# One layer of a hybrid diffusion backbone: weights split into high and low parts in operations of 1024 columns, in two pairs of buffers

## The chip, the cores and the metric

The kernel runs on one core of a Trainium2 chip. The metric is the time of one execution in device microseconds (us), lower is better. Engines are named as in the profile: PE (TensorE matmul), PEld (its weight load), DVE (VectorE), ACT (ScalarE), POOL (GpSimd), SP (the queue that issues most DMAs).

## What is computed

One layer is run over 128 context tokens and 256 latent tokens (384 in all) of width 2048, in fp32:

```python
h = rmsnorm(x, g_pre_mix) * (1.0 + sc1) + sh1
q, k, v, f, uv, ga, gf, gc = split(h @ w_in)              # 2048 x 10752
merged = (sigmoid(ga) * (attention(q, k, v) @ w_br_a)
        + sigmoid(gf) * (fourier(f) @ w_br_f)
        + sigmoid(gc) * (gating(uv) @ w_br_c))
x = x + gt1 * rmsnorm(merged @ w_out, g_post_mix)
h = rmsnorm(x, g_pre_mlp) * (1.0 + sc2) + sh2
x = x + gt2 * rmsnorm(square(relu(h @ w1)) @ w2, g_post_mlp)   # 2048 x 8192 x 2048
# sh1, sc1, gt1, sh2, sc2, gt2 = silu(c) @ w_ada + b_ada, for the context's and the latents' vector
```

## The kernel before

**Every weight is read once and used in three products.** A product is made in the type fp32r from two parts of each operand, a rounded high part and the remainder (low part): high weight by high activation, high by low, low by high. The two parts of a weight are made on the chip by `split` (line 70): ACT rounds it (`whi`, line 71), DVE subtracts the rounded value (`wlo`, recorded under line 65, the helper `tt`).

**The stream.** All weights stand in one list, `stream`, in the order of use. An entry is 128 partitions by up to 1024 columns (512 KB), read by one DMA of SP into a buffer `raw` (line 96, three buffers, `R_BUFS`; at the start six others, the tiles `era` and `erb`). Entries marked "W" are split and multiplied by PE; entries marked "D" are multiplied with the conditioning vector on DVE (line 274, four operations of 512 columns; early ones on PE, line 248), and are needed only later. D entries stand between W entries in three places: corrections for v and f in the first part of the projections, then 96 entries of `w_ada` beside the gates, branches and the output projection (positions 62 to 196 of `main`), then 32 in the MLP.

**Halves.** A W entry gives two halves of 512 columns. Each half has its own pair of tiles, `whi` and `wlo` (lines 117 and 118, four of each, `H_BUFS`). `next_half` (line 124) hands out the next half, and first calls `advance` until two more halves stand ready behind it. So in the program's order the split of an entry stands just ahead of the matmuls on the first half of the entry before it. The four tiles are used in turn: a half's split waits until PE has finished the half four places earlier, and the `raw` buffer becomes free, and with it the DMA three entries later, when the second subtraction is done.

**Blocks.** `blockA` multiplies with the weight as the stationary operand (a half is 12 matmuls of 384 or 386 columns), `blockB` with the weight as the moving one (9 matmuls of 512 columns). Behind each half a `slot` emits one to three pieces of other work (evacuations, attention, norms), so these stand in the queues of ACT, DVE and PE between the splits. Each engine works its queue in order. The first 24 entries of the MLP are only 512 columns wide and give one half each; between them DVE and ACT make the MLP's input (lines 1175 to 1186).

Of the kernel before, what the change touches and what calls it, by code (L numbers as in the profile page):

```python
# [14 lines left out]
F32R = mybir.dt.float32r  # L15
# [4 lines left out]
P = 128  # L20
# [15 lines left out]
def hybrid_layer_kernel(ctx: ExitStack, tc: tile.TileContext, I: dict, O: dict):  # L36
# [5 lines left out]
    wp = ctx.enter_context(tc.tile_pool(name="wp", bufs=3))  # L42
# [21 lines left out]
    def tt(eng, out, a, b, op):  # L64
        eng.tensor_tensor(out=out, in0=a, in1=b, op=op)  # L65

    def f32(ap):
        return ap.bitcast(F32)

    def split(full, hi, lo):  # L70
        nc.scalar.copy(out=hi, in_=full)  # L71
        tt(nc.vector, lo, full, f32(hi), ALU.subtract)

    R_BUFS = 3
    H_BUFS = 4
    RED_AFTER = 14
    ADD_AFTER = 7
    N_EARLY = 6
    stream = []
    state = {"done": 0, "dma": 0}  # L80
    halves = deque()
# [9 lines left out]
    def emit_dma(i):  # L91
        _, w, k0, nk, c0, nc_ = stream[i][:6]
        if i < early["n"]:
            raw = early_raw[i % N_EARLY]
        else:
            raw = wp.tile([P, 1024], F32, tag="raw", name=f"raw{i}", bufs=R_BUFS)
        nc.sync.dma_start(
            out=raw[:, :nk * nc_].rearrange("p (k n) -> p k n", k=nk),
            in_=ktv(w)[:, k0:k0 + nk, c0:c0 + nc_],
        )  # L100
        raws[i] = raw

    def advance():
        i = state["done"]
        if i < early["n"]:
            last_dma = min(i + N_EARLY - 1, early["n"] + R_BUFS - 1)
        else:
            last_dma = i + R_BUFS - 1
        while state["dma"] <= min(last_dma, len(stream) - 1):
            emit_dma(state["dma"])  # L110
            state["dma"] += 1
        e = stream[i]
        state["done"] += 1
        raw = raws.pop(i)
        if e[0] == "W":
            for hf in range(e[3] * e[5] // 512):
                hi = wp.tile([P, 512], F32R, tag="whi", name=f"whi{i}_{hf}", bufs=H_BUFS)
                lo = wp.tile([P, 512], F32R, tag="wlo", name=f"wlo{i}_{hf}", bufs=H_BUFS)
                split(raw[:, hf * 512:(hf + 1) * 512], hi, lo)
                halves.append((hi, lo))  # L120
        else:
            e[6](raw)

    def next_half():
        while not halves:
            advance()
        h = halves.popleft()
        while len(halves) < H_BUFS - 2 and state["done"] < len(stream):
            advance()
        return h  # L130

# [21 lines left out]
    def WB(w, k0, nkt, c0):  # L153
        return [("W", w, k, 2, c0, 512) for k in range(k0, k0 + nkt, 2)]
# [282 lines left out]
    for qd in range(4):  # L437
# [6 lines left out]
        for n in range(4):  # L444
            e = WB(w2, 16 * qd, KT, 512 * n)
# [160 lines left out]
    def blockA(name, src, nkt, evac, k_off=0, width=TOK):  # L606
        ps = [acc_tile(f"{name}_{n}") for n in range(2)]
        for k in range(0, nkt, 2):
            h = next_half()
            mmA(ps, h, k_off + k, src, k == 0, k == nkt - 2, width)  # L610
            slot()
        late.extend(evac(ps))

    def blockB(name, src, nkt, evac, k_off=0):
        ps = [acc_tile(f"{name}_{t}") for t in range(NT)]
        for k in range(nkt):
            h = next_half()
            mmB(ps, h, k_off + k, src, k == 0, k == nkt - 1)
            slot()
        late.extend(evac(ps))  # L620
# [50 lines left out]
    for ch in SCHED:  # L671
        if ch in "sW":
            advance()
            for _ in range(3):
                if xtask:
                    xtask.popleft()()
        elif ch in "Cc":
            consume()
            if ch == "C":
                consume()  # L680
        elif ch == "h" and todo:
            todo.popleft()()
        elif ch == "H":
            while todo:
                todo.popleft()()
# [447 lines left out]
    for k in range(0, KT - 2, 2):  # L1133
        mmA(ps7, next_half(), k, src_m, k == 0, False)
        slot()
    flush()
    hi, lo = (x.rearrange("p (k n) -> p k n", k=2) for x in next_half())
# [166 lines left out]
    for t in range(NT):  # L1304
# [4 lines left out]
        for n in range(4):  # L1309
            c = slice(512 * n, 512 * (n + 1))  # L1310
            o = accn[:, t, c].rearrange("p (k n) -> p k n", n=P)
# [50 lines left out]
```

## Time and profile before

| | |
|---|---|
| median of 3 runs | 2242.39 us (2242.16 to 2245.22) |
| span of the profiled execution | 2241.9 us |
| PE busy | 2168.3 us (97%) |
| DVE busy | 1458.1 us (65%) |
| ACT busy | 814.8 us (36%) |
| bytes moved by DMA | 387.29 MB, 173 GB/s in the mean |

The profile gives one execution; its span reaches from the first to the last instruction and lies 0.5 us below the median of the runs. Busy time of an engine is a union: a matmul is recorded at some 340 ns, though the next one starts 175 ns after it, so the number of matmuls in a stretch says more about PE than its busy share. "Idle before" an instruction is time in which its engine waited for what is named behind the arrow.

### The profile page before, as it was taken

Reading aid. Unit: us, or ns where it says so; the run is one execution under the profiler, and the core shown is the slowest. Engines: PE = TensorE matmul, PEld = TensorE weight load, DVE = VectorE, ACT = ScalarE, POOL = GpSimd, SP = SyncE. Lnnn points to the kernel's source line nnn. Section 1 sums busy time; section 2 is a strip of 40 time slices with the busy share of each in tenths; the row PEclk is TensorE's granted clock in tenths of the full one; section 3 lists DMA queues with packets and bytes.
Section 4 is the critical chain, followed back from the end, with each engine's and each line's share of the span. In section 5 each row is a group of like instructions: output and inputs, shape, how many; then the busy total and the mean of one; then the engine's idle time right before and its main releaser. Section 6 shows DMA issues by size and latency. Waiting matters only on the chain.

```text
span 2241.9 us, 30677 instructions
## 1 busy us (share of the span) xinstructions
PE 2168.3 (97%) x11479; PEld 1988.6 (89%) x11479; DVE 1458.1 (65%) x2331; ACT 814.8 (36%) x1602; POOL 252.6 (11%) x167
## 2 busy tenths in 40 slices
PE   7999899999999998999999999999999999999998
PEld 3679888999899998998989988899889998899986
DVE  4445675558998898989977577787444444345454
ACT  3332334533223232323245443344333443334441
POOL 0000221011222122212212001111000000000000
PEclk9999999999999999999999999999999999999999
DMA  8897753336666765666634466665444444444452
GB/s 309 288 314 232 198 161 123 103 116 196 201 195 194 212 207 168 201 203 224 218 102 134 126 191 200 205 188 174 127 132 124 128 125 129 126 130 123 123 175 88
DMA packets 284405, 387.29 MB, mean 173 GB/s; under 512 B 16156, under 2 KB 184304, under 8 KB 283872
## 3 DMA queue, kind: packets, MB, share of 16 engines
q1 hardware_dynamic: 275952, 372.82, 53.6%
q10 hardware_dynamic: 6192, 6.77, 1.0%
q0 software_dynamic: 2112, 5.74, 0.9%
q8 instruction: 90, 1.47, 0.3%
q14 instruction: 59, 0.48, 0.1%
HBM read 377.94 MB, written 8.26 MB: 172 GB/s over the span
## 4 chain that ended last, share of the span: by engine, by line
PE 75%; DVE 9%; DMA 8%; issue 5%; ACT 1%; POOL 1%; DVEq 0%; ACTq 0%; POOLq 0%; SPq 0%
PE m L576 7%; PE m L577 7%; PE m L575 7%; PE z L599 7%; PE z L600 7%; PE z L598 7%; DMA raw<-in_w_in_dram 4%; DVE wlo L65 4%; PE g L577 3%; PE g L575 3%; PE g L576 3%; DVE adr L274 3%; DMA raw<-in_w_ada_dram 2%; PE sc L248 2%; PE ew L598 1%
## 5 line engine op out<-in xcount | busy, mean ns | idle before, releaser
L65 DVE TENSOR_TENSOR wlo<-raw,whi 128x512 fp32r<-128x512 f32 x908 | 649.7, 734 | 573.5 <-ACT whi L71 566.2
L71 ACT CAST whi<-raw 128x512 fp32r<-128x512 f32 x908 | 547.8, 620 | 1102.8 <-PE z L600 262.0
L598 PE MATMUL z<-whi,ff 128*128 128x512 f32 x720 | 280.1, 389 | 0.0
L599 PE MATMUL z<-wlo,ff 128*128 128x512 f32 x720 | 280.1, 389 | 0.0
L600 PE MATMUL z<-whi,ff 128*128 128x512 f32 x720 | 280.1, 389 | 0.0
L274 DVE SCALAR_TENSOR_TENSOR adr<-raw,silT,adr 128x512 f32<-128x512 f32 x360 | 266.8, 801 | 15.5 <-DMA raw<-in_w_ada_dram 15.4
L577 PE MATMUL g<-hA,wlo 128*128 128x384 f32 x768 | 261.5, 341 | 15.6 <-DVE wlo L65 15.3
L575 PE MATMUL g<-hA,whi 128*128 128x384 f32 x768 | 260.9, 340 | 10.5 <-ACT whi L71 10.5
L576 PE MATMUL g<-hA,whi 128*128 128x384 f32 x768 | 259.4, 338 | 0.0
L575 PE MATMUL m<-h2a,whi 128*128 128x386 f32 x512 | 175.1, 342 | 2.1 <-ACT h2a L1181 2.1
L576 PE MATMUL m<-h2a,whi 128*128 128x386 f32 x512 | 174.3, 340 | 1.1 <-DVE h2a L1185 1.0
L577 PE MATMUL m<-h2a,wlo 128*128 128x386 f32 x512 | 173.8, 339 | 0.0
L577 PEld LDWEIGHTS g<-hA,wlo 128*128 128x128 f32 x768 | 146.2, 190 | 22.1 <-DVE wlo L65 22.1
L600 PEld LDWEIGHTS z<-whi,ff 128*128 128x128 f32 x720 | 135.1, 188 | 28.0
L598 PEld LDWEIGHTS z<-whi,ff 128*128 128x128 f32 x720 | 135.1, 188 | 27.9
L599 PEld LDWEIGHTS z<-wlo,ff 128*128 128x128 f32 x720 | 135.1, 188 | 27.9
L575 PEld LDWEIGHTS g<-hA,whi 128*128 128x128 f32 x768 | 146.1, 190 | 11.5 <-ACT whi L71 11.4
L576 PEld LDWEIGHTS g<-hA,whi 128*128 128x128 f32 x768 | 146.2, 190 | 0.0
L281 POOL PARTITION_ALL_REDUCE adr<-adr x24 | 87.4, 3640 | 302.8 <-DVE adr L274 235.1
L576 PEld LDWEIGHTS m<-h2a,whi 128*128 128x128 f32 x512 | 97.3, 190 | 2.3 <-DVE h2a L1185 2.1
L575 PEld LDWEIGHTS m<-h2a,whi 128*128 128x128 f32 x512 | 97.1, 190 | 2.4 <-ACT h2a L1181 2.3
L577 PEld LDWEIGHTS m<-h2a,wlo 128*128 128x128 f32 x512 | 96.9, 189 | 0.0
(343 smaller groups left out, 3824.6 us busy)
## 6 DMA issues: line engine op xcount, KB each, us to landing
raw<-in_w_mlp_dram SPq DMA_DIRECT2D x244, 512.0 KB, 3.7
raw<-in_w_in_dram SPq DMA_DIRECT2D x156, 512.0 KB, 3.8
raw<-in_w_ada_dram SPq DMA_DIRECT2D x128, 512.0 KB, 4.5
erb<-in_w_ada_dram SPq DMA_DIRECT2D x37, 512.0 KB, 5.5
raw<-in_w_out_dram SPq DMA_DIRECT2D x32, 512.0 KB, 4.2
era<-in_w_ada_dram SPq DMA_DIRECT2D x27, 512.0 KB, 5.1
era<-in_w_in_dram SPq DMA_DIRECT2D x20, 512.0 KB, 5.4
raw<-in_w_br_a_dram SPq DMA_DIRECT2D x16, 512.0 KB, 3.6
```

The costliest lines, as they stand in the source:

```text
L65: eng.tensor_tensor(out=out, in0=a, in1=b, op=op)
L71: nc.scalar.copy(out=hi, in_=full)
L248: nc.tensor.matmul(ps[g:g + 2, :wd], silT[:, :, k], r, start=k < 4, stop=k >= KT - 4)
L274: nc.vector.scalar_tensor_tensor(out=acc[v], in0=r, scalar=vec[:, v, k:k + 1], in1=acc[v], op0=ALU.mult, op1=ALU.add)
L281: nc.gpsimd.partition_all_reduce(out, acc, P, bass_isa.ReduceOp.add)
L575: nc.tensor.matmul(out, wh, xh, start=start, stop=False)
L576: nc.tensor.matmul(out, wh, xl, start=False, stop=False)
L577: nc.tensor.matmul(out, wl, xh, start=False, stop=stop)
L598: nc.tensor.matmul(ps[t], xh, hi, start=first, stop=False)
L599: nc.tensor.matmul(ps[t], xh, lo, start=False, stop=False)
L600: nc.tensor.matmul(ps[t], xl, hi, start=False, stop=last_)
```

## The change

An entry of 1024 columns is split whole: one rounding on ACT and one subtraction on DVE, into one pair of tiles of 1024 columns. There are two such pairs in place of four of 512; they take the same memory. The two halves that are handed out are views of one pair. Two entries of 512 columns share a pair, and each is split for itself into its half of it. The number of halves that stand ready ahead is 2 as before, under a name of its own.

```diff
-    H_BUFS = 4
+    H_TILES = 2
+    AHEAD = 2
...
         if e[0] == "W":
-            for hf in range(e[3] * e[5] // 512):
-                hi = wp.tile([P, 512], F32R, tag="whi", name=f"whi{i}_{hf}", bufs=H_BUFS)
-                lo = wp.tile([P, 512], F32R, tag="wlo", name=f"wlo{i}_{hf}", bufs=H_BUFS)
-                split(raw[:, hf * 512:(hf + 1) * 512], hi, lo)
-                halves.append((hi, lo))
+            n = e[3] * e[5]
+            if "pair" in state:
+                pair, o = state.pop("pair"), 512
+            else:
+                pair, o = [wp.tile([P, 1024], F32R, tag=t, name=f"{t}{i}", bufs=H_TILES) for t in ("whi", "wlo")], 0
+                if n == 512:
+                    state["pair"] = pair
+            split(raw[:, :n], *(t[:, o:o + n] for t in pair))
+            for c in range(o, o + n, 512):
+                halves.append(tuple(t[:, c:c + 512] for t in pair))
...
-        while len(halves) < H_BUFS - 2 and state["done"] < len(stream):
+        while len(halves) < AHEAD and state["done"] < len(stream):
```

DVE's queue beside the gates and branches (`wlo190_0` is the first half of entry 190, `adr` the sums of a D entry, `sig` the gated branches), before:

```order
L65 TENSOR_TENSOR wlo190_0_4721<-raw190_4674,whi190_0_4720 128x512
L65 TENSOR_TENSOR wlo190_1_4725<-raw190_4674,whi190_1_4724 128x512
L271 TENSOR_SCALAR adr_4313<-raw191_4712,silT_89 128x512 x2
L274 SCALAR_TENSOR_TENSOR adr_4313<-raw191_4712,silT_89,adr_4313 128x512 x2
L65 TENSOR_TENSOR wlo192_0_4768<-raw192_4718,whi192_0_4767 128x512
L65 TENSOR_TENSOR wlo192_1_4772<-raw192_4718,whi192_1_4771 128x512
L65 TENSOR_TENSOR sig00_4382<-b0_1_0_4672,sig00_4382 128x384
L65 TENSOR_TENSOR sig01_4396<-b0_1_1_4673,sig01_4396 128x384
L274 SCALAR_TENSOR_TENSOR adr_4313<-raw193_4759,silT_89,adr_4313 128x512 x4
```

and now:

```order
L65 TENSOR_TENSOR wlo190_4313<-raw190_4270,whi190_4312 128x1024
L277 TENSOR_SCALAR adr_3945<-raw191_4304,silT_89 128x512 x2
L280 SCALAR_TENSOR_TENSOR adr_3945<-raw191_4304,silT_89,adr_3945 128x512 x2
L65 TENSOR_TENSOR wlo192_4356<-raw192_4310,whi192_4355 128x1024
L65 TENSOR_TENSOR sig00_4006<-b0_1_0_4268,sig00_4006 128x384
L65 TENSOR_TENSOR sig01_4020<-b0_1_1_4269,sig01_4020 128x384
L280 SCALAR_TENSOR_TENSOR adr_3945<-raw193_4347,silT_89,adr_3945 128x512 x4
```

Two rows have become one of twice the width; nothing else has moved. ACT's queue changes in the same way, from 1556 rows to 1086, as DVE's from 2020 to 1550.

PE's queue at the border between the two halves of entry 192 (lines 575 to 577 are the three products of `mm3`, now 581 to 583), before:

```order
L576 MATMUL b2_1_1_4802<-oC_3836,whi192_0_4767 128x384
L577 MATMUL b2_1_1_4802<-oC_3836,wlo192_0_4768 128x384
L575 MATMUL b2_1_0_4801<-oC_3836,whi192_1_4771 128x384
L576 MATMUL b2_1_0_4801<-oC_3836,whi192_1_4771 128x384
L577 MATMUL b2_1_0_4801<-oC_3836,wlo192_1_4772 128x384
```

and now:

```order
L582 MATMUL b2_1_1_4386<-oC_3516,whi192_4355 128x384
L583 MATMUL b2_1_1_4386<-oC_3516,wlo192_4356 128x384
L581 MATMUL b2_1_0_4385<-oC_3516,whi192_4355 128x384
L582 MATMUL b2_1_0_4385<-oC_3516,whi192_4355 128x384
L583 MATMUL b2_1_0_4385<-oC_3516,wlo192_4356 128x384
```

The order of the matmuls is the same; both halves now read one pair of tiles, which becomes free behind the last matmul of the second half.

ACT's queue at the first entries of the MLP, which are 512 columns wide (lines 1181 and 1187 make the MLP's input `h2a`), before:

```order
L71 CAST whi410_0_10194<-raw410_10098 128x512
L71 CAST whi411_0_10216<-raw411_10116 128x512
L1181 ACTIVATE h2a_10158<-xT2_10168,A2_92 128x128
L1181 ACTIVATE h2a_10158<-xT2_10168,A2_92 128x256
L71 CAST whi412_0_10238<-raw412_10192 128x512
```

and now:

```order
L71 CAST whi410_9264<-raw410_9170 128x512
L71 CAST whi410_9264<-raw411_9188 128x512
L1187 ACTIVATE h2a_9228<-xT2_9238,A2_92 128x128
L1187 ACTIVATE h2a_9228<-xT2_9238,A2_92 128x256
L71 CAST whi412_9306<-raw412_9262 128x512
```

The instructions are the same; entries 410 and 411 now share the pair `whi410`.

## Rows read from the trace of the kernel before

**Rows 1.** Windows by stretch: length, PE, PEld, DVE, ACT, POOL; clock, DMA share, GB/s.

```profile
168.00:290.00 122.00, 111.94 (x619) 107.39 (x618) 79.25 (x134) 37.22 (x71) 19.64 (x22) 0.97 0.71 211
290.00:550.00 260.00, 259.57 (x1453) 245.37 (x1452) 159.53 (x287) 107.57 (x227) 31.15 (x26) 1.00 0.45 138
550.00:870.00 320.00, 305.58 (x1711) 299.21 (x1710) 287.28 (x399) 94.00 (x173) 83.29 (x45) 0.99 0.66 200
870.00:1120.00 250.00, 231.31 (x1277) 224.75 (x1278) 221.29 (x319) 74.54 (x139) 57.48 (x31) 0.97 0.66 203
1120.00:1240.00 120.00, 113.34 (x644) 110.03 (x643) 83.98 (x158) 59.99 (x137) 21.23 (x20) 0.97 0.39 118
1240.00:1570.00 330.00, 330.00 (x1714) 307.33 (x1713) 244.23 (x367) 134.33 (x272) 36.55 (x14) 1.00 0.59 182
1570.00:2180.00 610.00, 610.00 (x3032) 551.76 (x3031) 278.92 (x440) 232.23 (x450) 0.00 (x0) 1.00 0.42 130
```

**Rows 2.** Windows inside a blockA and a blockB stretch of the MLP.

```profile
1736.00:1792.00 56.00, 56.00 (x319) 56.00 (x318) 27.95 (x47) 25.89 (x58) 0.00 (x0) 1.00 0.41 123
1848.00:1904.00 56.00, 56.00 (x249) 46.37 (x248) 22.01 (x33) 17.21 (x28) 0.00 (x0) 1.00 0.41 128
```

**Rows 3.** Waits of DVE, 550 to 1120 us: us in total, times, longest.

```profile
DVE wlo L65 <- ACT whi L71: 33.4, 49, 2.5
DVE adr L274 <- DMA raw<-in_w_ada_dram: 14.5, 18, 2.4
```

**Rows 4.** Waits of DVE, then of ACT, 168 to 290 us.

```profile
DVE wlo L65 <- ACT whi L71: 26.7, 9, 7.2
...
ACT whi L71 <- DMA raw<-in_w_in_dram: 60.3, 14, 8.2
```

**Rows 5.** Groups by shape, ACT, whole span: busy us, mean ns | idle before.

```profile
L71 ACT CAST whi<-raw 128x512 fp32r<-128x512 f32 x908 | 547.8, 620 | 1102.8 <-PE z L600 262.0 <-DMA raw<-in_w_in_dram 211.0 <-PE m L576 199.5
...
L546 ACT CAST hA<-bx 128x384 fp32r<-128x384 f32 x16 | 8.2, 514 | 14.6 <-DVE bx L544 14.0
```

**Rows 6.** Groups by shape, DVE, whole span: an operation of 1024 columns.

```profile
L65 DVE TENSOR_TENSOR a<-a,bg 128x1024 f32<-128x1024 f32 x8 | 9.7, 1218 | 0.1
```

**Rows 7.** Timeline, DVE, about 629 us: start, us, instruction, [idle before].

```profile
628.85 1.29 DVE L65 TENSOR_TENSOR wlo<-raw,whi 128x512 fp32r<-128x512 f32 x2 [1.35 <-ACT whi L71]
630.06 1.02 DVE L65 TENSOR_TENSOR sig<-b,sig 128x384 f32<-128x384 f32 x2
```

**Rows 8.** Chain that ended last, 621 to 632 us: start, us, what.

```profile
628.20 0.63 ACT whi L71
...
629.46 0.69 DVE wlo L65
```

**Rows 9.** Groups by shape, DVE, 550 to 870 us, then 870 to 1120 us.

```profile
L65 DVE TENSOR_TENSOR wlo<-raw,whi 128x512 fp32r<-128x512 f32 x140 | 104.4, 784 | 20.9 <-ACT whi L71 19.5 <-PE g L577 0.8
...
L65 DVE TENSOR_TENSOR wlo<-raw,whi 128x512 fp32r<-128x512 f32 x108 | 83.8, 817 | 14.7 <-ACT whi L71 13.9 <-PE g L577 0.5
```

**Rows 10.** Timeline, ACT, then DVE, in a blockA of the MLP.

```profile
1751.37 0.62 ACT L71 CAST whi<-raw 128x512 fp32r<-128x512 f32 x1 [1.52 <-PE m L576]
...
1752.02 0.69 DVE L65 TENSOR_TENSOR wlo<-raw,whi 128x512 fp32r<-128x512 f32 x1 [1.44 <-ACT whi L71]
1752.63 1.02 DVE L65 TENSOR_TENSOR z<-m,r 128x384 f32<-128x384 f32 x2
```

**Rows 11.** Timeline, DVE, where D entries stand in the MLP.

```profile
1501.13 2.73 DVE L274 SCALAR_TENSOR_TENSOR ada<-raw,silT,ada 128x512 f32<-128x512 f32 x4
1503.79 1.28 DVE L65 TENSOR_TENSOR wlo<-raw,whi 128x512 fp32r<-128x512 f32 x2
```

**Rows 12.** Chain that ended last, 656 to 668 us.

```profile
661.99 0.69 DVE wlo L65
...
662.73 0.69 PE g L577
663.41 0.32 PE g L575
```

## The prediction

> **What bounds the kernel now.** I read the windows by stretch first. PE sets the pace where it starts a matmul of 384 columns every 175 ns (56 us / 319) and one of 512 every 225 ns (56 us / 249) [rows 2]. From 290 to 550 us and from 1240 to 2180 us it does: its busy time is the whole stretch [rows 1], and no wait ends there that a faster ACT or DVE could shorten. From 550 to 1120 us (gates, branches, output projection, with the D entries between) it does not: 1711 + 1277 matmuls at 175 ns are 523 us of work in 570, so 47 us are lost. From 168 to 290 us the same count gives 619 x 0.175 = 108 of 122, so 14 are lost. In the first of these two, DVE is busy 287.28 of 320 and 221.29 of 250 us [rows 1], nearly full but not quite: the waits say that 49 times a subtraction stood waiting for its rounding on ACT, 33.4 us in all, and 18 times the sums of a D entry waited for their transfer, 14.5 us [rows 3]. In the second DVE has time to spare, and ACT waits for DMA, 60.3 us in 14 waits [rows 4].
>
> So there are two stretches in which the splits are on the path, and they are on it in two ways: as load on a nearly full DVE, and as latency from a transfer's landing to the release of its buffer `raw`, since with three buffers the DMA of the third entry after it starts only then. The change makes the load smaller and the latency longer. The forecast is which of the two weighs more.
>
> **The change part by part.** First the two new operations, which this trace does not show.
>
> The rounding of 1024 columns: 514 ns for 384 columns and 620 ns for 512 [rows 5] make 106 ns for 128 columns, so 620 + 4 x 106 = 1.04 us. It can't cost more than the two that it replaces, which start 0.52 us apart and end after 1.14 us. I take 1.05, between them and near the first, which is the same operation.
>
> The subtraction of 1024 columns: DVE has an operation of that line and width, at 1.218 us [rows 6]. Two of 512 back to back take 1.29 us from start to end, and the next instruction starts 1.21 us after the first [rows 7], so 0.08 us of an operation's end lie under the next one. With 1.22 us the next would start after 1.14. The bounds are 1.14 and 1.21: the saving is between 0 and 0.07 us an entry, and I take 0.07, since row and operation are alike.
>
> From these, four prices. They are worked out on the entry at 628 us, whose rounding starts at 628.20, whose second subtraction ends at 630.15 [rows 8], and behind which DVE goes on at 630.06 [rows 7]:
> - DVE is behind and the rounding is long done: 1.14 in place of 1.21 us, a saving of **0.07 us**.
> - DVE waits for the rounding: before, DVE is free 1.86 us after the rounding starts, since the second rounding hides under the first subtraction. Now 1.05 + 0.02 + 1.14 = 2.21, a loss of **0.35 us**, for DVE and for the release of `raw`.
> - PE waits for the first half, DVE was waiting too: before, 0.63 + 0.02 + 0.69 = 1.34 us; now 1.05 + 0.02 + 1.22 = 2.29, a loss of **0.95 us**, once, each time that PE takes over the path.
> - PE waits for the first half and DVE was behind: 1.22 against 0.69, a loss of **0.53 us**, likewise.
>
> *550 to 1120 us.* There are (140 + 108) / 2 = 124 entries [rows 9]. Of these, 49 waited for the rounding [rows 3] (a few of the 49 are second halves, which I price alike) and pay 0.35: +17.2 us. The other 75 save 0.07: -5.3. What else is queued on DVE behind the longer wait is the next D entry; 18 of these waited for their own transfer, 14.5 us in all [rows 3], and a D entry whose transfer is already under way takes up to 0.35 us of a delay: between 0 and -6.3 us; I take half, -3. At the end of the stretch, where PE has the path again, between 0.53 and 0.95: +0.7. Sum +9.6.
>
> *168 to 290 us.* 21 entries, 9 of which waited for the rounding [rows 4]: +3.2; the other 12: -0.8; PE's own last wait: +0.95, since DVE is not behind there. Sum +3.3.
>
> *290 to 550 and 1240 to 2180 us.* Here the new release rule counts. A split now waits until PE has finished both halves of the entry two places earlier, so it starts when PE starts the entry between: 24 x 175 ns = 4.2 us in blockA, 18 x 225 ns = 4.05 in blockB [rows 2]. At 1751 us the rounding follows PE's release at once, the subtraction 0.65 us later, and behind it stand evacuations of 0.5 us each [rows 10]. Now release to ready is 1.05 + 0.02 + 1.22 = 2.3 us, which leaves 1.75 us for other work that stands ahead on ACT or DVE. Before, the first half had 2.1 us more, because it did not wait for the second. The hardest place is the MLP with D entries: one D holds DVE 2.66 us (1501.13 to 1503.79) [rows 11], but it stands ahead of the split and need not wait for PE, so it runs while PE is still in the entry before; two entries (8.4 us) hold two subtractions, one D and three evacuations of 0.5, 2.28 + 2.66 + 1.5 = 6.4 us. I take 0, and keep +16 (the 1714 matmuls from 1240 to 1570 us [rows 1] are some 80 entries, at a fifth of a us each) for a rival below.
>
> *1120 to 1240 us.* The 24 entries of 512 columns keep their operations; only the first of each two waits for one half more of PE. PE loses time there to the making of its input (644 x 0.175 = 113 of 120 us) [rows 1]. +0.7, between 0 and +2. The stretch before 168 us and the end: 0.
>
> **The sum**: 9.6 + 3.3 + 0 + 0.7 = +13.6 us on the span of 2241.9, 2255.5; the median of the runs lies 0.5 above the span: **2256 us**.
>
> What the rows show of DVE is that it is 90% busy and yet waits 49 times for ACT [rows 1, 3]. The Trainium skill has a rule for each side of this, in Perfetto Trace Analysis, section Optimizing Scalar/DVE Operations: larger operations help if the engine is saturated, at about 60 ns saved for an operation less on DVE and about 93 on ScalarE; but if the engines "aren't saturated, but are causing bubbles on other engines, breaking up instructions may allow work to be completed sooner". By the first alone the stretch would gain 124 x 0.06 = 7.4 us, an estimate from the page's figure. The trace agrees with the size (0.07 here) and with the second rule at 628 us, where half the width let DVE start 0.4 us earlier.
>
> **The rivals.**
>
> *Load decides (faster).* If DVE is the pacemaker from 550 to 1120 us and its waits are gaps that close by themselves, all 124 entries save 0.07 and nobody pays: -8.7 us, some -1 us before 290: 2233. For it: 287 of 320 us busy. Against it: the gaps are there, and the rounding that ends them is itself waiting for a transfer that DVE's own release started. It wins if fewer than 15 of the 124 splits still wait for the rounding (15 x 0.35 = 75 x 0.07).
>
> *The two cancel (no change).* If two thirds of the 49 + 9 waits go, because transfers land sooner when they are issued less close together, 20 x 0.35 = 7 us and PE's own 1.6 stand against 0.07 x 125 = 8.7 us: 2242.
>
> *The two pairs are too few (slower still).* If the full-rate stretches begin to stall, from 1240 to 1570 us first, +16 us there come on top: 2272, and more if PE's clock follows. After its wait at 658 to 662 us PE ran at 0.32 us a matmul instead of 0.17 [rows 12], the lower of its two levels, 1.2 in place of 2.4 GHz. Against it: the 1.75 us of room.
>
> **How the numbers follow.** Load decides 0.14 (2229 to 2237); cancel 0.18 (2238 to 2246); the forecast 0.55 (2247 to 2266); too few pairs 0.13 (2266 to 2285). Faster by over 0.2% (4.5 us, about what a measurement of this kernel can tell from no change) is the first alone, 0.14; within 0.2% the second, 0.18; slower 0.68. The range leaves out half of the first and half of the last: 2236 to 2274.
>
> **What would show it.** Right: the DVE waits for the rounding from 550 to 1120 us stay near 49 and their sum rises from 33 to some 54 us (0.42 for each); fewer than 2988 matmuls per 570 us there; the stretch ends some 9 us later, the one before 290 us some 3 us later; PE starts in the MLP at the same rates, 319 and 249 in 56 us; rounding near 1.05 and subtraction near 1.22 us. Wrong: subtraction clearly under 1.2 us, or fewer than 15 waits for the rounding (faster); PE idle anywhere in 290 to 550 or 1240 to 2180 us (slower than said); a granted clock below that of [rows 1].

## The result, and the profile after

The changed kernel takes **2253.61 us** (median of 4 runs, 2250.82 to 2256.21), the kernel before 2242.27 beside it: a ratio of **1.0053, 95% interval 1.0037 to 1.0069**, 8 to 15 us slower. The forecast was 2256, in a range from 2236 to 2274. The profiled execution has a span of 2252.4 us, 10.5 more than before.

The same windows as in [rows 1], of the kernel after:

```profile
168.00:290.00 122.00, 113.20 (x632) 109.80 (x632) 78.58 (x113) 35.31 (x48) 20.99 (x22) 0.97 0.72 213
290.00:550.00 260.00, 257.57 (x1435) 242.13 (x1434) 149.89 (x230) 98.91 (x172) 29.49 (x26) 1.00 0.45 137
550.00:870.00 320.00, 301.75 (x1695) 293.71 (x1693) 279.45 (x331) 86.80 (x103) 79.26 (x44) 1.00 0.65 198
870.00:1120.00 250.00, 228.42 (x1262) 220.82 (x1262) 210.79 (x264) 65.20 (x79) 53.22 (x30) 0.98 0.64 199
...
1736.00:1792.00 56.00, 56.00 (x320) 56.00 (x319) 26.17 (x35) 21.31 (x37) 0.00 (x0) 1.00 0.41 122
1848.00:1904.00 56.00, 56.00 (x248) 46.36 (x248) 20.56 (x21) 17.15 (x21) 0.00 (x0) 1.00 0.43 132
```

From 550 to 1120 us PE now starts 1695 + 1262 = 2957 matmuls in place of 2988, DVE is 18 us less busy there, and PE loses all the same. Its granted clock is no lower there (1.00 and 0.98, before 0.99 and 0.97), so a slower clock is not what the change costs. The two MLP windows run at the old rate [rows 2]. Waits of DVE and PE from 550 to 1120 us, after (us in total, times, longest):

```profile
DVE wlo L65 <- ACT whi L71: 62.2, 62, 2.9
...
DVE adr L280 <- DMA raw<-in_w_ada_dram: 8.3, 11, 1.3
...
PE g L583 <- DVE wlo L65: 20.6, 21, 2.1
PE g L581 <- ACT whi L71: 8.1, 2, 7.0
PE y L583 <- DVE wlo L65: 7.0, 8, 1.7
PE b L583 <- DVE wlo L65: 3.2, 3, 1.6
```

and those of PE in the same stretch before, which stand in no row ahead:

```profile
PE g L577 <- DVE wlo L65: 15.3, 15, 3.7
PE g L575 <- ACT whi L71: 10.5, 2, 8.6
PE y L577 <- DVE wlo L65: 5.4, 7, 1.8
PE b L577 <- DVE wlo L65: 0.7, 1, 0.7
PE y L575 <- ACT whi L71: 0.6, 1, 0.6
```

DVE waits for the rounding 62 times and 62.2 us, against 49 and 33.4 [rows 3]; the D sums' own waits fall from 14.5 to 8.3 us. PE waits for a subtraction 32 times and 30.8 us, against 23 and 21.4: 9.4 us more. Its waits for a rounding fall from 11.1 to 8.1, so that all of its waits grow by 6.4 us. The two new operations, ACT and then DVE, mean ns of one in the third number:

```profile
L71 ACT CAST whi<-raw 128x1024 fp32r<-128x1024 f32 x442 | 464.7, 1052 | 1152.6 <-PE z L606 312.5 <-DMA raw<-in_w_in_dram 231.5 <-PE m L582 221.9
...
L65 DVE TENSOR_TENSOR wlo<-era,whi 128x1024 fp32r<-128x1024 f32 x20 | 24.5, 1226 | 29.6 <-ACT whi L71 29.2
```

These 20 subtractions are of early entries; the 442 later ones have a mean of 1300 ns (before, with 512 columns, 734 against 688 for the same early ones). And the place where the forecast priced them [rows 7, 8], the timeline of ACT and of DVE after:

```profile
631.69 1.05 ACT L71 CAST whi<-raw 128x1024 fp32r<-128x1024 f32 x1 [2.37 <-DMA raw<-in_w_br_c_dram]
...
632.78 1.23 DVE L65 TENSOR_TENSOR wlo<-raw,whi 128x1024 fp32r<-128x1024 f32 x1 [2.20 <-ACT whi L71]
633.92 1.02 DVE L65 TENSOR_TENSOR sig<-b,sig 128x384 f32<-128x384 f32 x2
```

From the rounding's start to the next instruction on DVE it is 633.92 - 631.69 = 2.23 us, where it was 1.86; from the subtraction's start 1.14. The forecast said 2.21 and 1.14.

### The profile page after: what moved, and what is told of

It reads as the page before. It is cut to its first block, busy times and chain, and to the rows that moved or that the text cites. A ratio compares the mean times of both kernels' runs of the same rounds, so it can differ in the third digit from the quotient of the medians.

```text
span 2252.4 us, 29037 instructions
## 1 busy us (share of the span) xinstructions
PE 2167.9 (96%) x11479; PEld 1984.2 (88%) x11479; DVE 1400.6 (62%) x1861; ACT 747.0 (33%) x1132; POOL 246.5 (11%) x167
## 4 chain that ended last, share of the span: by engine, by line
PE 71%; DVE 13%; DMA 9%; issue 4%; ACT 3%; POOL 1%; ACTq 0%; DVEq 0%; POOLq 0%
PE m L582 8%; PE m L583 8%; PE m L581 8%; PE z L605 7%; PE z L606 7%; PE z L604 7%; DVE wlo L65 5%; DMA raw<-in_w_in_dram 5%; DVE adr L280 4%; PE g L583 2%; PE g L582 2%; PE g L581 2%; ACT whi L71 2%; PE sc L254 2%; DMA raw<-in_w_out_dram 1%
## 5 line engine op out<-in xcount | busy, mean ns | idle before, releaser
L65 DVE TENSOR_TENSOR wlo<-raw,whi 128x1024 fp32r<-128x1024 f32 (+1 forms) x466 | 593.5, 1276 | 667.7 <-ACT whi L71 667.0
L71 ACT CAST whi<-raw 128x1024 fp32r<-128x1024 f32 (+1 forms) x466 | 479.3, 1029 | 1165.8 <-PE z L606 312.5
L280 DVE SCALAR_TENSOR_TENSOR adr<-raw,silT,adr 128x512 f32<-128x512 f32 x360 | 275.1, 824 | 8.8 <-DMA raw<-in_w_ada_dram 8.3
```

Of the source, the lines that this page charges most:

```text
L280: nc.vector.scalar_tensor_tensor(out=acc[v], in0=r, scalar=vec[:, v, k:k + 1], in1=acc[v], op0=ALU.mult, op1=ALU.add)
```

## Where the time went, by stage

To place the 10.5 us, the table takes the start of the same matmul in every trace and gives the time from mark to mark: the first for `k` (187 us in the kernel before), the first for `v` (293), the 577th for `g` (564), the 600th for `y` (1119), the 768th for `m` (1304), the 1700th for `z` (1960), the first for the last tile `zl` (2200). The kernels below the second row belong to the experiments; "wide" marks stages whose entries are split 1024 columns at a time.

| kernel | k to v | v to g | g to y | y to m | m to z | z to zl | waits of DVE, g to y | waits of PE, g to y |
|---|---|---|---|---|---|---|---|---|
| before | 106.5 | 270.6 | 555.0 | 184.5 | 656.5 | 240.1 | 33.1 | 32.5 |
| after (all wide) | 104.4 | 274.8 | 561.1 | 184.5 | 656.9 | 242.1 | 59.9 | 39.2 |
| e2_fine (none wide) | 100.4 | 271.5 | 554.6 | 185.4 | 656.5 | 240.2 | 37.5 | 32.6 |
| e3 (rounding wide) | 106.7 | 272.8 | 565.3 | 184.0 | 656.5 | 241.3 | 53.9 | 38.6 |
| e4 (subtraction wide) | 109.6 | 274.2 | 564.0 | 184.4 | 657.1 | 242.5 | 64.2 | 41.4 |
| e10 (g to y not wide) | 100.8 | 273.0 | 558.9 | 186.0 | 656.9 | 242.1 | 42.7 | 34.3 |
| e11 (only g to y wide) | 103.1 | 272.3 | 560.1 | 183.8 | 656.5 | 240.2 | 55.9 | 35.4 |
| e12 (only up to g wide) | 101.2 | 273.0 | 555.2 | 183.9 | 656.5 | 240.2 | 32.4 | 35.3 |
| e13 (only from m on wide) | 105.1 | 271.5 | 554.7 | 183.4 | 656.9 | 242.1 | 36.9 | 31.5 |
| e7 (half buffers) | 91.7 | 270.7 | 534.9 | 184.2 | 656.5 | 240.1 | 29.8 | 19.7 |
| e8 (two transfers) | 96.1 | 270.7 | 537.9 | 184.2 | 656.5 | 240.1 | 30.2 | 21.5 |
| e9 (half buffers, two pairs) | 93.9 | 271.4 | 537.7 | 185.4 | 656.5 | 240.2 | 37.5 | 22.4 |

The last two columns are what DVE waits for the rounding, and what PE waits for anything, between the marks of `g` and `y`, in us. PE starts the same 2903 matmuls there in every kernel.

After against before: -2.1, +4.2, **+6.1**, 0, +0.4, +2.0, in sum +10.6. Each row is one execution, and executions of one kernel differ: the twelve of e12 run from 2239.9 to 2254.3 us, and the traced one is its fastest, 8 us under its median. The first column varies by 6 us among kernels that split alike there (106.5, 100.4, 103.1, 105.1), so nothing under some 5 us can be read from it; the columns from `m` on repeat to a tenth among kernels that split alike there.

## Experiments

Theory A is the forecast's: latency. A wide split hands over its result later, and DVE, the release of `raw` and PE wait for that. The rivals: the wider pairs, whose two halves are released together, are what costs; or one of the two operations alone is.

**Fine splits into the wide pairs.** The pairs and their release stay as in the kernel after, the operations go back to 512 columns.

```diff
-            split(raw[:, :n], *(t[:, o:o + n] for t in pair))
+            for c in range(0, n, 512):
+                split(raw[:, c:c + 512], *(t[:, o + c:o + c + 512] for t in pair))
```

> The changed kernel with one part undone: the two pairs of 1024 columns stay, and with them the rule that a pair becomes free only behind its second half, but each half is rounded and subtracted for itself, 512 columns at a time. Theory A (latency: the rounding of 1024 columns stands whole ahead of the subtraction, 0.35 us for each of some 50 entries that wait for it between 550 and 1120 us): back to the kernel before, 2242 to 2245 us. Theory B (release: two pairs are too few, the wait for PE's second half costs the time): stays at 2251 to 2255 us, with the roundings between 550 and 1120 us waiting for PE as often as in the changed kernel (some 20 times).

Measured: 2241.59 us, ratio 1.0007 (0.9992 to 1.0022). From 550 to 1120 us DVE waits for the rounding about as often and as long as before:

```profile
DVE wlo L65 <- ACT whi L71: 37.8, 50, 2.9
```

The pairs alone cost nothing that can be measured, though ACT's roundings wait for PE there 26 times, against 23 in the kernel after; the width of the operations does cost. This is the run that separates the two halves of the change, and the case for latency.

**One operation wide, the other not.** The next two kernels keep the pairs and widen only the rounding, or only the subtraction.

```diff
-            split(raw[:, :n], *(t[:, o:o + n] for t in pair))
+            nc.scalar.copy(out=pair[0][:, o:o + n], in_=raw[:, :n])
+            for c in range(0, n, 512):
+                tt(nc.vector, pair[1][:, o + c:o + c + 512], raw[:, c:c + 512], f32(pair[0][:, o + c:o + c + 512]), ALU.subtract)
```

> The changed kernel with the subtraction alone cut in two: one rounding of 1024 columns, two subtractions of 512, two pairs. Theory A: the subtraction starts as late as in the changed kernel and DVE does not save its 0.07 us an entry, but PE's first half is ready 0.5 us sooner; DVE's waits cost 0.42 us each, 62 of them, so 2254 to 2260 us. Theory B: as the changed kernel, 2251 to 2255. If the width of the subtraction were what costs (PE waits 1.22 in place of 0.69 us for its first half): 2243 to 2247.

Measured: 2257.36 us, ratio 1.0080 (1.0064 to 1.0096).

```diff
-            split(raw[:, :n], *(t[:, o:o + n] for t in pair))
+            for c in range(0, n, 512):
+                nc.scalar.copy(out=pair[0][:, o + c:o + c + 512], in_=raw[:, c:c + 512])
+            tt(nc.vector, pair[1][:, o:o + n], raw[:, :n], f32(pair[0][:, o:o + n]), ALU.subtract)
```

> The changed kernel with the rounding alone cut in two: two roundings of 512 columns, one subtraction of 1024 that waits for both, two pairs. Theory A: both roundings end 1.14 us after the first starts, 0.09 later than the one of 1024, on some 60 waiting entries: 5 us more than the changed kernel, 2255 to 2261 us. Theory B: as the changed kernel, 2251 to 2255.

Measured: 2257.91 us, ratio 1.0077 (1.0056 to 1.0099). DVE's waits for the rounding, 550 to 1120 us, with the wide rounding and then with the wide subtraction (two kernels, hence two line numbers):

```profile
DVE wlo L65 <- ACT whi L124: 54.0, 60, 2.9
```

```profile
DVE wlo L65 <- ACT whi L125: 65.2, 60, 3.2
```

Each operation alone makes nearly the whole wait: a subtraction can start no sooner than its rounding, and a wide one no sooner than both. Both times are where theory A had them. Both kernels lie 5 to 6 us above the kernel after by their ratios (4 by the medians), though the intervals (up to 1.0069 there, from 1.0056 and 1.0064 here) overlap a little. The fewer and wider instructions may give that back, where 124 x 0.07 = 8.7 had been reckoned, but it is not shown: with the wide rounding PE waits as long from `g` to `y` as in the kernel after (38.6 and 39.2 us), and the stage takes 4 us more.

**Where the width costs.** Two kernels split the stream at the middle stage, `g` to `y`: fine there and wide elsewhere (e10), and the opposite (e11, with `not` before the condition).

```diff
-            split(raw[:, :n], *(t[:, o:o + n] for t in pair))
+            wd = 512 if 186 <= i < 400 else n
+            for c in range(0, n, wd):
+                split(raw[:, c:c + wd], *(t[:, o + c:o + c + wd] for t in pair))
```

> The kernel after, but entries 186 to 399 of the stream (those that are split from 550 to 1120 us) are split in two operations of 512 columns each, into the same two pairs; all others stay 1024 wide. Theory A by place (the cost of the wide operations lies in 550 to 1120 us and nearly nothing elsewhere): most of the 10 us comes back, 2241 to 2246 us; the profile stands within 3 us of the kernel before at 1120 us and keeps the 1 to 2 us that the last two blocks of z lose. Rival (the loss is spread over all places, as 0.35 us for each of some entries everywhere): 2247 to 2251 us.

Measured: 2249.83 us, ratio 1.0042 (1.0027 to 1.0057). Not what theory A by place said, but inside the rival's range; the loss is not all in the middle.

> The opposite of the kernel with fine splits in the middle: entries 186 to 399 (550 to 1120 us) are split 1024 columns wide, all others in two operations of 512. Theory A by place: nearly the whole loss is here, 2248 to 2254 us, 7 to 10 us of it made between 550 and 1120 us. Rival (the loss is spread over all places): 2243 to 2247 us.

Measured: 2247.79 us, ratio 1.0037 (1.0024 to 1.0051), between the ranges of theory A by place and of the rival. In its trace the middle is 5.1 us longer than before, where theory A had 7 to 10, and DVE's and PE's waits there are those of the kernel after:

```profile
DVE wlo L65 <- ACT whi L71: 56.3, 62, 2.3
...
PE g L585 <- DVE wlo L65: 19.8, 21, 2.4
PE y L585 <- DVE wlo L65: 7.0, 6, 1.9
...
PE b L585 <- DVE wlo L65: 3.1, 3, 1.6
```

So two more kernels were wide in one of the outer parts alone (`i >= 186`, or `i < 400`, as the condition for 512).

> The kernel after, with entries before number 186 of the stream (split until 550 us) 1024 columns wide and all later ones in two operations of 512. By the terms of the forecast (+3.3 from 168 to 290 us, nothing from 290 to 550): 2243 to 2247 us. By the profile of the kernel after (one wait of the attention for DVE 1.2 us longer at 400 to 460 us, about zero from 168 to 290 us): 2240 to 2244 us. By the median of the kernel that is fine in the middle alone, if its +9 us are real and made here: 2246 to 2251 us.

Measured: 2248.06 us, ratio 1.0032 (1.0018 to 1.0046): the third of its ranges, above what the forecast's terms and the profile gave.

> The kernel after, with entries from number 400 of the stream on (the MLP and the last of the output projection) 1024 columns wide and all earlier ones in two operations of 512. By the terms of the forecast (+0.7 from 1120 to 1240 us, 0 in the MLP): 2241 to 2244 us. By the profile of the kernel after (PE stands twice for a subtraction between 2140 and 2180 us): 2 us more than the kernel with fine splits everywhere (2241.6), 2242 to 2246 us, with both stalls of PE in the profile. If the +9 us of the kernel that is fine in the middle alone are made here: 2246 to 2251 us, and waits of PE for the split all along the MLP.

Measured: 2244.41 us, ratio 1.0020 (1.0007 to 1.0033): the second range, with both stalls of PE, as the profile of after has them:

```profile
PE z L607 <- DVE wlo L65: 1.4, 2, 0.7
```

Against the fine kernel's 1.0007 the three parts cost 5.6, 6.7 and 2.9 us, each within some 5 us either way; they sum to 15 and the whole measured 10, which their intervals allow. The medians can't divide 10 us among three places. The table can in part: wide splits cost some 1 to 3 us from `v` to `g` (273.0, 273.0 and 274.8 against 271.5, 272.3, 271.5 with the same pairs), 5 to 6 from `g` to `y` (560.1 and 561.1 against 554.6, 555.2 and 554.7; e10, fine there, has 558.9 for a reason that the trace doesn't give), and 2.3 from `m` to `zl`, each time the same.

Two of these have a single cause that can be seen. From 290 to 550 us PE waits once for the attention's scores `s`, which stand on DVE behind a split: first before, then the fine kernel, then after:

```profile
PE pa L889 <- DVE s L880: 0.4, 1, 0.4
```

```profile
PE pa L896 <- DVE s L887: 0.9, 1, 0.9
```

```profile
PE pa L895 <- DVE s L886: 1.6, 1, 1.6
```

It is 1.6 us in each trace that is wide there (after, e10, e12) and 0.9 in each that is fine with the same pairs (e2, e11, e13). And at 2152 us (2186 likewise), the timeline of ACT, DVE and PE after, at a border between blocks of `z`:

```profile
2148.69 0.60 ACT L1249 ACTIVATE z<-accn 128x512 f32<-128x512 f32 x1 [1.36 <-DVE accn L65]
...
2149.32 1.13 ACT L71 CAST wzB<-raw 128x512 fp32r<-128x512 f32 x2
2150.36 1.05 ACT L71 CAST whi<-raw 128x1024 fp32r<-128x1024 f32 x1
...
2151.44 1.23 DVE L65 TENSOR_TENSOR wlo<-raw,whi 128x1024 fp32r<-128x1024 f32 x1
...
2152.72 0.50 PE L605 MATMUL z<-wlo,ff 128*128 128x512 f32 x1 [0.70 <-DVE wlo L65]
```

The rounding stands behind two evacuations, which go back and forth between ACT and DVE, and two other roundings. The subtraction ends at 2152.67, and PE, which needs it for its second matmul, has stood 0.70 us. From the 1700th for `z` to `zl` PE starts a matmul more than 0.3 us after the one before only here and at 2186 us (after 1.10 and 0.34 us, then 1.09 and 0.34, where it is 0.23 otherwise): together 2.0 us, the whole of that column.

**Half the transfer.** If time from landing to release is what counts, making it shorter than in the kernel before should gain. Six `raw` buffers of 512 columns, each with its own transfer of 256 KB, take the place of three of 1024 in the kernel before; the splits are its own. `Halved`, which is not shown, holds an entry's two tiles and hands a slice to the one that it lies in; the early entries are left as they are.

```diff
...
-            raw = wp.tile([P, 1024], F32, tag="raw", name=f"raw{i}", bufs=R_BUFS)
...
+            raw = Halved()
+            hk = 512 // nc_
+            for q in range(nk // hk):
+                t = wp.tile([P, 512], F32, tag="raw", name=f"raw{i}_{q}", bufs=2 * R_BUFS)
+                nc.sync.dma_start(
+                    out=t.rearrange("p (k n) -> p k n", k=hk),
+                    in_=ktv(w)[:, k0 + q * hk:k0 + (q + 1) * hk, c0:c0 + nc_],
+                )
+                raw.t.append(t)
```

> The kernel before, with the buffer raw (behind the first entries) cut in halves: six buffers of 512 columns in place of three of 1024, each with a DMA of its own of 256 KB, so a half's transfer starts when the subtraction of that half is done, and its rounding when that half has landed. It asks whether the path from a landing to the next transfer sets the pace between 550 and 1120 us. Theory A: it does, and the stretch gets shorter: 2228 to 2240 us. If DVE's load alone sets the pace there: 2240 to 2245. If transfers of half the size are worse for DMA: above 2246, with longer times to landing for the same bytes.

Measured: **2207.41 us, ratio 0.9858 (0.9842 to 0.9873)**, 33 us less than before, well beyond the 2228 that theory A had as its far end, and the fastest kernel here. Its windows of 168 to 290 and 550 to 1120 us:

```profile
168.00:290.00 122.00, 120.86 (x694) 117.70 (x693) 95.59 (x159) 44.32 (x84) 23.17 (x25) 1.00 0.75 232
...
550.00:870.00 320.00, 305.38 (x1723) 302.79 (x1722) 287.32 (x409) 101.58 (x178) 80.59 (x44) 0.98 0.66 203
870.00:1120.00 250.00, 241.30 (x1366) 236.37 (x1365) 223.04 (x335) 82.60 (x149) 57.55 (x29) 0.99 0.66 207
```

From `k` to `v` it takes 91.7 us (106.5 before), from `g` to `y` 534.9 (555.0); elsewhere nothing changes by more than 0.3 us.

**Landing or release.** The same transfers into the three whole buffers tell which of the two it was.

```diff
-        nc.sync.dma_start(
-            out=raw[:, :nk * nc_].rearrange("p (k n) -> p k n", k=nk),
-            in_=ktv(w)[:, k0:k0 + nk, c0:c0 + nc_],
-        )
+        hk = 512 // nc_ if i >= early["n"] else nk
+        for q in range(0, nk, hk):
+            nc.sync.dma_start(
+                out=raw[:, q * nc_:(q + hk) * nc_].rearrange("p (k n) -> p k n", k=hk),
+                in_=ktv(w)[:, k0 + q:k0 + q + hk, c0:c0 + nc_],
+            )
```

> The kernel before, where each of the three raw buffers of 1024 columns is filled by two transfers of 256 KB in place of one of 512 KB, one for each half; the buffer is still released whole, after its second subtraction. It stands against the kernel with raw in six halves of 512 columns (2207.4 us), which has the same transfers and releases each half for itself. Theory A (release decides: in the kernel before the next transfer starts only when both subtractions are done, and that waiting is what costs): little is won, 2236 to 2246 us, and from 550 to 1120 us ACT still waits for transfers as before, the sums of a D entry 10 us and more. Rival C (landing decides: the first rounding can start when half of the data is there, about 1.3 us sooner): nearly all of the gain of the half buffers comes here too, 2205 to 2218 us, and the waits of the D sums fall under 3 us. Rival D (more and smaller transfers are themselves dearer): 2246 us and more.

Measured: 2218.53 us, ratio 0.9907 (0.9886 to 0.9929): half a us above what rival C said, far below A. The D sums still wait for their transfers, 4.0 us (C said under 3; 14.5 before). Some two thirds of the gain (22 of 33 us) come with the first half being there sooner, one third with its release; in the stages it is 10.4 of 14.8 and 17.1 of 20.1 us, in a traced execution that is 3 us under the median. From `g` to `y` the first half lands 3.8 us after its issue and the second 0.7 us after the first (medians of the 48 of 208 pairs whose landing the trace tells), where a whole transfer took 4.6 before (54 of 208). Theory A had the right chain, from landing to release, and its wrong end: the start of the rounding weighs more than the release.

The Trainium skill (SBUF — State Buffer, section The DMA setup-cost knee) advises the largest single transfer where DMA is the bound, since each has a fixed cost. Here two of 256 KB beat one of 512 KB at no lower rate (203 GB/s from 550 to 870 us in the windows of the half buffers, 200 before [rows 1]). The measurement decides, for a kernel whose first consumer needs half of the bytes.

**Both together.** The half buffers, with fine splits into the two wide pairs.

> The kernel after with raw in six halves of 512 columns, each half landed and split for itself (512 columns) into the two pairs of 1024. It stands against the kernel before with the same halves, which took 2207.4 us. Theory A (the release rule of two wide pairs is nearly harmless; what cost time was the width of the two operations): within 5 us of that, 2203 to 2213 us, a ratio of 0.983 to 0.988 against before. Rival B (with transfers no longer late, the pairs become the next thing that is waited for, since both halves of a pair are released together): 2214 to 2230 us, and ACT's rounding waits for PE (whi for g, b, y) longer than in the kernel with four pairs of 512.

Measured: 2214.39 us, ratio 0.9883 (0.9861 to 0.9905), 7 us above the half buffers with four pairs, so B by a hair (the intervals still overlap, from 0.9861 to 0.9873). ACT's waits for PE from 550 to 1120 us, with four pairs of 512 and then with two of 1024:

```profile
ACT whi L81 <- PE g L594: 65.3, 52, 2.0
...
ACT whi L81 <- PE b L594: 44.7, 34, 1.5
...
ACT whi L81 <- PE y L594: 20.9, 17, 1.5
```

```profile
ACT whi L81 <- PE g L601: 138.0, 51, 9.6
ACT whi L81 <- PE b L601: 53.7, 20, 3.1
...
ACT whi L81 <- PE y L601: 49.0, 21, 3.3
```

Once the weights are there sooner, ACT waits longer for the joint release of a pair: 241 us against 131. With whole transfers the same step, from the kernel before to the fine kernel, raises ACT's waits for PE only from 55 to 64 us, which fits that the pairs alone cost nothing there.

## Why the prediction was right, and where it was not

**The sign, the mechanism and the total** held: 2256 said, 2253.6 measured. Latency outweighs load. The fine kernel (1.0007) shows that the width costs, the two half-wide ones that either operation suffices. The four prices stand on operations that came out as worked out, though only the first two prices were seen whole: 1.052 us for the rounding (1.05 said), 1.226 for the subtraction (1.22), 1.14 from its start to the next (1.14), 2.23 from rounding to the next on DVE (2.21).

**550 to 1120 us: +9.6 said, 5 to 6 measured.** The count of waits rose, 62 in place of about 49, and their sum is 62.2 us, not 54. By the step as it was written, that would be dearer still: 62 x 0.35 less 62 x 0.07 is 17 us, the D sums take 6.2 of it (14.5 - 8.3; 3 was taken, 6.3 the bound), and 0.7 comes on top: 12. The failed step is that all 49 waits of DVE were priced as waits on the path. PE waits for a subtraction 23 times in that stretch before and 32 after, so about half of DVE's waits end while PE still has a split half to work on. PE's waits grew by 9.4 us; 31 matmuls fewer at 175 ns are 5.4 us, and the stage is 6.1 longer. The last two columns of the table bear out that the waits of PE are the ones to price: with half buffers and two pairs DVE waits longer for the rounding than before (37.5 us against 33.1), PE shorter (22.4 against 32.5), and the stage is 17 us shorter; over the twelve kernels the stage grows nearly in the order of PE's waits. No run changed the one wait and left the other alone.

**168 to 290 us: +3.3 said, not found.** The stage is 2 us shorter in the trace of after, and three traces that are wide there (104.4, 100.8, 101.2) don't stand above four that are not (106.5, 100.4, 103.1, 105.1); the two with one operation wide have 106.7 and 109.6. The term is smaller than what this stage varies by, which comes with the landing of the transfers and which I can't explain further.

**290 to 550 us: 0 said, +4.2 measured in after**, of which 1.2 is the attention's wait for DVE (0.4 to 1.6 us) and 0.6 a single wait of PE for a split (`g`, in that trace alone). I had looked only at PE's wait for the split; what else is queued on DVE behind a wide subtraction, and who waits for that, was left out for this stretch. In the fine kernel with the same pairs it is +0.9.

**1240 us to the end: 0 said, +2.4 measured**, repeated in all three kernels that are wide there. The rival "two pairs too few" had the mechanism, the release of a whole pair and 1.75 us of room for other work, and the wrong place: the full-rate stretch with D entries runs as before, but at the borders of the last two `z` blocks the work ahead of the rounding on ACT takes more than the room. Two stalls of PE are 2.0 of these 2.4 us. The release alone does not make them: the kernels that are fine there, with the same pairs, have none and take 240.2 us from `z` to `zl`, as before. The timeline there was not read for the prediction.

**1120 to 1240 us: +0.7 said, 0 measured** (184.5 both times, from `y` to `m`).

So a total that is right to 3 us came from two terms that were some 4 us too large and two zeros that were 2 to 4 us too small: the sign and the mechanism are earned, the closeness of the total is luck. The rival "load decides" fell with the waits, which stayed far above 15 (by the forecast's own prices the balance is at 21, since 21 x 0.35 = 103 x 0.07); "the two cancel" with the interval, which begins at 1.0037. What stays open: how the 10 us divide to better than a few us, since kernels that do the same in a stage differ by as much in one execution.

The rule weighed there (Perfetto Trace Analysis in the Trainium skill, section Optimizing Scalar/DVE Operations) is borne out on its second side: an engine that is 90% busy and still waits 49 times is not saturated, another engine (PE) waits for it 23 times, and the narrower operations win by 0.5%.

## What to carry to other kernels

Widening an operation saves a little per instruction (0.07 us was reckoned here) and delays its first result by the whole added width (0.4 to 0.5 us here); before doing it, count how often the consumer behind it waits in the present trace, and price the waits of the engine that sets the pace, not those of the engine in between. Make the unit that lands, is worked on and is released the same as the unit that is consumed: here half the transfer and half the buffer gave 1.4%, and twice the operation took 0.5%. A stretch said to have room needs its borders read too, since the room was smallest here where blocks end and evacuations queue ahead.

## What was not expected of the hardware

Splitting a transfer of 512 KB into two of 256 KB cost nothing that shows. Their median times from issue to landing from 550 to 1120 us, in the kernel with whole buffers before and in the one with two transfers each:

```profile
raw<-in_w_ada_dram SPq DMA_DIRECT2D x87, 512.0 KB, 4.7
raw<-in_w_in_dram SPq DMA_DIRECT2D x72, 512.0 KB, 4.4
raw<-in_w_out_dram SPq DMA_DIRECT2D x29, 512.0 KB, 4.9
```

```profile
raw<-in_w_ada_dram SPq DMA_DIRECT2D x172, 256.0 KB, 3.8
raw<-in_w_in_dram SPq DMA_DIRECT2D x142, 256.0 KB, 4.0
raw<-in_w_out_dram SPq DMA_DIRECT2D x64, 256.0 KB, 3.9
```

Half of the bytes take 0.4 to 1.0 us less, far from half of the time. Yet with two under way at once the second half follows the first by 0.7 us, so the pair is there 4.4 us after its first issue, no later than the whole was (4.6), and ACT has the first half sooner.
